# Binary cross-entropy on one core: a flat walk in 64 KiB runs over two SBUF rings, float32 results in place, every transfer on the GpSimd queue

## The chip, the cores and the metric

The kernel runs on one core of a Trainium2 chip. The metric is device time in microseconds (us), the median of several executions.

## The reference

```python
pred   = uniform(0.01, 0.99, (8192, 8192)).astype(float32)
target = randint(0, 2, (8192, 8192)).astype(float32)      # only 0.0 and 1.0

eps = 1e-7
pred = clip(pred, eps, 1 - eps)
out  = -(target * log(pred) + (1 - target) * log(1 - pred))
```

As the target is 0 or 1, the result is `-log|p - 1 + t|`: one logarithm is enough. Both kernels use that.

Two arrays of 268 MB are read and one of 268 MB is written: 805 MB in all, and very little arithmetic.

## The kernel before

It takes 64 blocks of 128 rows x 8192 columns. A row of a block is 32 KiB of contiguous float32. There are three buffers for pred, two for the target (cast to bf16 by the DMA) and two for the result (fp16, cast to float32 by the DMA).

```python
    def ops(bi, rows, r0, g0, t_p, t_t):
        t_o = pool_o.tile([P, F], fp16, name="t_o", tag="t_o")
        p_sl = t_p[:rows]
        nc.vector.scalar_tensor_tensor(               # p - 1 + t
            out=p_sl, in0=p_sl, scalar=1.0, in1=t_t[:rows], op0=sub, op1=add)
        nc.scalar.activation(out=p_sl, in_=p_sl, func=Square)
        nc.scalar.activation(out=p_sl, in_=p_sl, func=Ln)
        nc.vector.tensor_scalar(out=t_o[:rows], in0=p_sl, scalar1=-0.5, ...)
        # the store is put off: emit_store() issues it on gpsimd two blocks later

    def ops_tail(...):                                # the last two blocks, in 4 and 8 pieces
        ...                                           # same four ops, float32 in place
            nc.sync.dma_start(out=out_f[...], in_=p_sl)      # tail stores: SP queue

    for bi in range(n_blk):
        ...
        if big and bi == 0:
            nc.sync.dma_start(out=t_p[:rows], in_=pred_f[...])    # first pred load: SP queue
        else:
            nc.gpsimd.dma_start(out=t_p[:rows], in_=pred_f[...])
        nc.gpsimd.dma_start(out=t_t[:rows], in_=target_f[...])
        if bi - 2 in pending:
            emit_store(bi - 2)
        ...                                           # ops() or ops_tail()
```

Of the kernel before, what the change touches and what calls it, by code (L numbers as in the profile page):

```python
# [1 line left out]

# [4 lines left out]


@with_exitstack
def kernel(  # L10
    ctx: ExitStack,
    tc: tile.TileContext,
    pred: bass.AP,
    target: bass.AP,
    out: bass.AP,
):
    nc = tc.nc
    fp32 = mybir.dt.float32
    fp16 = mybir.dt.float16
    bf16 = mybir.dt.bfloat16  # L20

    P = nc.NUM_PARTITIONS

    pred_f = pred.flatten_outer_dims()
    target_f = target.flatten_outer_dims()
    out_f = out.flatten_outer_dims()

    R, C = pred_f.shape

    F = 8192 if C % 8192 == 0 else C  # L30
    n_col = C // F
    n_row = (R + P - 1) // P
    n_blk = n_row * n_col

    big = (R % P == 0) and n_blk >= 8 and F == 8192

    sub = mybir.AluOpType.subtract
    add = mybir.AluOpType.add
    mult = mybir.AluOpType.mult

    Square = mybir.ActivationFunctionType.Square
    Ln = mybir.ActivationFunctionType.Ln

    pool_p = ctx.enter_context(tc.tile_pool(name="bce_p", bufs=3 if big else 2))
    pool_t = ctx.enter_context(tc.tile_pool(name="bce_t", bufs=2))
    pool_o = ctx.enter_context(tc.tile_pool(name="bce_o", bufs=2))
    pool_w = ctx.enter_context(tc.tile_pool(name="bce_w", bufs=1))

    warm = pool_w.tile([1, 8], fp32, name="warm", tag="warm")
    nc.vector.memset(warm, 1.0)  # L50
    nc.scalar.activation(out=warm, in_=warm, func=Ln)  # L51

    lb = n_blk - 1
    slb = n_blk - 2

    pending: dict[int, list] = {}

    def emit_store(b: int, n: int | None = None):
        lst = pending[b]
        n = len(lst) if n is None else n  # L60
        for _ in range(n):
            dram, sl = lst.pop(0)
            nc.gpsimd.dma_start(out=dram, in_=sl)  # L63
        if not lst:
            del pending[b]

    def ops(bi, rows, r0, g0, t_p, t_t):
        t_o = pool_o.tile([P, F], fp16, name="t_o", tag="t_o")
        p_sl = t_p[:rows]
        nc.vector.scalar_tensor_tensor(  # L70
            out=p_sl, in0=p_sl, scalar=1.0, in1=t_t[:rows], op0=sub, op1=add
        )
        nc.scalar.activation(out=p_sl, in_=p_sl, func=Square)  # L73
        nc.scalar.activation(out=p_sl, in_=p_sl, func=Ln)  # L74
        nc.vector.tensor_scalar(  # L75
            out=t_o[:rows], in0=p_sl, scalar1=-0.5, scalar2=None, op0=mult
        )
        pending.setdefault(bi, []).append(
            (out_f[r0 : r0 + rows, g0 : g0 + F], t_o[:rows])
        )  # L80

    def ops_tail(rows, r0, g0, t_p, t_t, nchunk):
        W = F // nchunk
        for k in range(nchunk):
            c0 = k * W
            p_sl = t_p[:rows, c0 : c0 + W]
            nc.vector.scalar_tensor_tensor(  # L87
                out=p_sl,
                in0=p_sl,
                scalar=1.0,  # L90
                in1=t_t[:rows, c0 : c0 + W],
                op0=sub,
                op1=add,
            )
            nc.scalar.activation(out=p_sl, in_=p_sl, func=Square)  # L95
            nc.scalar.activation(out=p_sl, in_=p_sl, func=Ln)  # L96
            nc.vector.tensor_scalar(  # L97
                out=p_sl, in0=p_sl, scalar1=-0.5, scalar2=None, op0=mult
            )
            nc.sync.dma_start(  # L100
                out=out_f[r0 : r0 + rows, g0 + c0 : g0 + c0 + W], in_=p_sl
            )

    for bi in range(n_blk):
        i, j = divmod(bi, n_col)
        r0 = i * P
        rows = min(P, R - r0)
        g0 = j * F

        t_p = pool_p.tile([P, F], fp32, name="t_p", tag="t_p")  # L110
        t_t = pool_t.tile([P, F], bf16 if big else fp32, name="t_t", tag="t_t")

        if big and bi == 0:
            nc.sync.dma_start(out=t_p[:rows], in_=pred_f[r0 : r0 + rows, g0 : g0 + F])
        else:
            nc.gpsimd.dma_start(out=t_p[:rows], in_=pred_f[r0 : r0 + rows, g0 : g0 + F])  # L116
        nc.gpsimd.dma_start(out=t_t[:rows], in_=target_f[r0 : r0 + rows, g0 : g0 + F])  # L117

        s = bi - 2
        if s in pending:  # L120
            emit_store(s)

        if big and bi == slb:
            ops_tail(rows, r0, g0, t_p, t_t, 4)
        elif big and bi == lb:
            ops_tail(rows, r0, g0, t_p, t_t, 8)
        else:
            ops(bi, rows, r0, g0, t_p, t_t)

    for b in sorted(pending):  # L130
        emit_store(b)


# [1 line left out]
_INS = ['pred', 'target']  # L135
_OUTS = [((8192, 8192), 'float32')]


# [23 lines left out]
```

## Time and profile before

| | |
|---|---|
| time, median of 3 | 1867.4 us (1867.38 to 1867.72) |
| DMA, share of the 16 engines' span (GpSimd queue) | 99.9% |
| DVE / ACT busy | 45% / 48% |
| HBM traffic | 805 MB, 432 GB/s |

The first thing to read is the page's summary: busy time of the engines, the DMA row over 40 equal slices (each digit is tenths of busy time), and the queues (packets, MB, share of 16 engines).

```profile
DVE 841.3 (45%) x149; ACT 903.3 (48%) x150; POOL 100.9 (5%) x193
...
DMA  9999999999999999999999999999999999999999
...
q0 software_dynamic: 27216, 658.52, 99.9%
q1 hardware_dynamic: 1872, 12.58, 1.7%
...
HBM read 536.87 MB, written 268.44 MB: 432 GB/s over the span
```

DMA is full in every slice while the engines are idle half of the time. The queue `q0` is GpSimd's; `q1` is SP's. The MB of a queue are counted on the receiving side, so a cast target counts half (658.52 + 12.58 = 671.1 MB are 268.4 of pred, 134.2 of target in bf16 and 268.4 of result); the HBM line has the true bytes.

The packet records of the trace (start, duration and size of each DMA packet) show how full the engines are. I take the 16th packet after a given one for the next of the same engine: one packet takes 1226 ns (median), and the 16th starts 1209.5 ns later in a pred load, 1208 ns in a target load, 1207 ns in a store. All of these move 32 KiB on the float32 side, so the narrow side of these casts bought no DMA time. A transfer has 9 packets per engine: 8 rows and one 4-byte semaphore write (3024 packets of 4 bytes on this queue, 189 x 16). That is 27216 = 189 transfers x 16 x 9.

The end: these are busy times by window (us; busy us of DVE, ACT and POOL; clock; DMA share; GB/s).

```profile
1855.00:1860.00 5.00, 0.69 (x1) 1.24 (x2) 0.00 (x0) 1.00 1.02 419
1860.00:1865.00 5.00, 0.00 (x0) 0.00 (x0) 0.00 (x0) 1.00 0.57 231
1865.00:1865.70 0.70, 0.00 (x0) 0.00 (x0) 0.00 (x0) 1.00 0.00 0
```

DMA stays full until shortly before the end: the last data packet ends at 1863.95 us.

### The profile page before, as it was taken

The page shows a single profiled execution, that of the slowest core. Times are in us where ns is not written, and L with a number is a line of the kernel's source. Part 1 is how long each engine was busy: PE and PEld are TensorE (multiplying, and loading weights), DVE is VectorE, ACT ScalarE, POOL GpSimd, SP SyncE. Part 2 cuts the span into 40 slices and gives each one's busy share as a digit, 9 for nine tenths or more (in the row PEclk, how much of TensorE's full clock was granted, in tenths as well). Part 3 has the DMA queues.
Part 4 walks back from the last instruction along what each step waited for, and adds up shares of the span by engine and source line. Part 5 has one row for each costly group of instructions (what it writes and reads, how often), then busy time and mean ns, then how long its engine had stood idle before and what let it go on. Part 6 is the DMA issues. An engine that isn't in the chain of part 4 may idle for free.

```text
span 1865.7 us, 804 instructions
## 1 busy us (share of the span) xinstructions
DVE 841.3 (45%) x149; ACT 903.3 (48%) x150; POOL 100.9 (5%) x193
## 2 busy tenths in 40 slices
DVE  2645344453443534435344353453534535345353
ACT  3653644535445354453544635446354463553654
POOL 0000000000000000000000000000000000000000
DMA  9999999999999999999999999999999999999999
GB/s 325 338 377 353 351 379 344 375 356 347 384 341 376 356 346 387 344 368 363 343 388 345 364 369 341 390 344 360 371 343 386 344 359 372 347 379 352 352 378 351
DMA packets 29093, 671.14 MB, mean 360 GB/s; under 512 B 3232, under 2 KB 3232, under 8 KB 4256
## 3 DMA queue, kind: packets, MB, share of 16 engines
q0 software_dynamic: 27216, 658.52, 99.9%
q1 hardware_dynamic: 1872, 12.58, 1.7%
q14 instruction: 5, 0.04, 0.0%
HBM read 536.87 MB, written 268.44 MB: 432 GB/s over the span
## 4 chain that ended last, share of the span: by engine, by line
DMA 80%; issue 14%; ACT 2%; DVE 2%; another core or an unknown queue 1%; POOL 0%; POOLq 0%; DVEq 0%; PEldq 0%
DMA t_t<-in_target_dram 80%; DVE t_p L70 1%; ACT t_p L96 1%; ACT t_p L95 1%; DVE t_o L75 0%; ACT t_p L73 0%; ACT t_p L74 0%; DVE t_p L87 0%; DVE t_p L97 0%; POOL t_p L116 0%; POOL out_dram L63 0%; POOLq L117 0%; POOL t_t L117 0%; POOLq L63 0%
## 5 line engine op out<-in xcount | busy, mean ns | idle before, releaser
L73 ACT ACTIVATE t_p<-t_p 128x8192 f32<-128x8192 f32 x62 | 435.8, 7029 | 923.6 <-DVE t_p L70 923.6
L75 DVE TENSOR_SCALAR t_o<-t_p 128x8192 f16<-128x8192 f32 x62 | 274.4, 4427 | 845.0 <-ACT t_p L74 845.0
L70 DVE SCALAR_TENSOR_TENSOR t_p<-t_p,t_t 128x8192 f32<-128x8192 f32 x62 | 538.9, 8693 | 144.8 <-DMA t_t<-in_target_dram 144.8
L74 ACT ACTIVATE t_p<-t_p 128x8192 f32<-128x8192 f32 x62 | 435.8, 7029 | 2.0
L63 POOL DMA_DIRECT2D out_dram<-t_o x62 | 33.4, 538 | 1121.9 <-DVE t_o L75 1101.2
L117 POOL DMA_DIRECT2D t_t<-in_target_dram x64 | 34.1, 533 | 581.5 <-DVE t_p L70 580.7
L116 POOL DMA_DIRECT2D t_p<-in_pred_dram x63 | 33.9, 537 | 0.3 <-issue 0.3
L95 ACT ACTIVATE t_p<-t_p 128x1024 f32<-128x1024 f32 (+1 forms) x12 | 15.6, 1327 | 26.5 <-DVE t_p L87 26.5
L87 DVE SCALAR_TENSOR_TENSOR t_p<-t_p,t_t 128x1024 f32<-128x1024 f32 (+1 forms) x12 | 18.4, 1575 | 17.2 <-DMA t_t<-in_target_dram 17.2
L96 ACT ACTIVATE t_p<-t_p 128x1024 f32<-128x1024 f32 (+1 forms) x12 | 15.6, 1330 | 0.1
L97 DVE TENSOR_SCALAR t_p<-t_p 128x1024 f32<-128x1024 f32 (+1 forms) x12 | 10.3, 868 | 7.9 <-ACT t_p L96 7.9
L51 ACT ACT_TABLE_LOAD x1 | 1.3, 1283 | 0.7 <-PEq L146 0.7
L50 DVE MEMSET warm<- 1x8 f32 x1 | 0.1, 65 | 0.8 <-PEq L146 0.8
L51 ACT ACTIVATE warm<-warm 1x8 f32<-1x8 f32 x1 | 0.2, 208 | 0.0
L146 POOL MEMSET const-float32-0.0<- 128x1 f32 x1 | 0.1, 100 | 0.2 <-issue 0.2
L146 POOL MEMSET const-bfloat16-1.0<- 128x1 bf16 x1 | 0.1, 102 | 0.0
L146 POOL MEMSET const-float32-1.0<- 128x1 f32 x1 | 0.1, 100 | 0.0
L146 POOL MEMSET const-uint8-127<- 128x1 uint8 x1 | 0.1, 100 | 0.0
## 6 DMA issues: line engine op xcount, KB each, us to landing
t_p<-in_pred_dram POOLq DMA_DIRECT2D x63, 4096.0 KB, 49.3
out_dram<-t_o POOLq DMA_DIRECT2D x62, 4096.0 KB, 40.1
t_t<-in_target_dram POOLq DMA_DIRECT2D x64, 2048.0 KB, 49.0
t_p<-in_pred_dram SPq DMA_DIRECT2D x1, 4096.0 KB, 19.6
out_dram<-t_p SPq DMA_DIRECT2D x4, 1024.0 KB, 27.3
out_dram<-t_p SPq DMA_DIRECT2D x8, 512.0 KB, 8.5
```

The costliest lines, as they stand in the source:

```text
L51: nc.scalar.activation(out=warm, in_=warm, func=Ln)
L63: nc.gpsimd.dma_start(out=dram, in_=sl)
L70: nc.vector.scalar_tensor_tensor(out=p_sl, in0=p_sl, scalar=1.0, in1=t_t[:rows], op0=sub, op1=add)
L73: nc.scalar.activation(out=p_sl, in_=p_sl, func=Square)
L74: nc.scalar.activation(out=p_sl, in_=p_sl, func=Ln)
L75: nc.vector.tensor_scalar(out=t_o[:rows], in0=p_sl, scalar1=-0.5, scalar2=None, op0=mult)
L87: nc.vector.scalar_tensor_tensor(out=p_sl, in0=p_sl, scalar=1.0, in1=t_t[:rows, c0 : c0 + W], op0=sub, op1=add,)
L95: nc.scalar.activation(out=p_sl, in_=p_sl, func=Square)
L96: nc.scalar.activation(out=p_sl, in_=p_sl, func=Ln)
L97: nc.vector.tensor_scalar(out=p_sl, in0=p_sl, scalar1=-0.5, scalar2=None, op0=mult)
L116: nc.gpsimd.dma_start(out=t_p[:rows], in_=pred_f[r0 : r0 + rows, g0 : g0 + F])
L117: nc.gpsimd.dma_start(out=t_t[:rows], in_=target_f[r0 : r0 + rows, g0 : g0 + F])
```

## The change

The intent: fewer and longer transfers (64 KiB runs where there were 32 KiB rows), no separate result buffer (float32 results in place, which also drops the fp16 rounding), the clip that the reference asks for, and one queue that holds all transfers in an order written by hand. The arrays are walked as flat memory. A chunk of width w is 128 runs of w elements, one per partition; widths go 4096, 4096, 8192, then 30 x 16384, then 8192, 4096, 2048, 1024, 1024. The ring for pred has 32768 columns, so it holds two large chunks.

```diff
+RING = 32768
+SUB = 2048
+    head = [4096, 4096, 8192]
+    tail = [8192, 4096, 2048, 1024, 1024]
+    big = 16384
 ...
+    ring_p = pool.tile([P, RING], fp32, name="ring_p", tag="ring_p")
+    ring_t = pool.tile([P, RING], bf16, name="ring_t", tag="ring_t")
 ...
+    def load(k):
+        c, w = at(k), widths[k]
+        nc.gpsimd.dma_start(out=ring_t[:, c : c + w], in_=dram(target_f, cols[k], w))
+        nc.gpsimd.dma_start(out=ring_p[:, c : c + w], in_=dram(pred_f, cols[k], w))
+    def store(k):
+        c, w = at(k), widths[k]
+        nc.gpsimd.dma_start(out=dram(out_f, cols[k], w), in_=ring_p[:, c : c + w])
+    def front(c, w):
+        p, t = ring_p[:, c : c + w], ring_t[:, c : c + w]
+        nc.vector.tensor_scalar(out=p, in0=p, scalar1=EPS, scalar2=1 - EPS, op0=Alu.max, op1=Alu.min)
+        nc.vector.scalar_tensor_tensor(out=p, in0=t, scalar=1.0, in1=p, op0=Alu.subtract, op1=Alu.add)
+        nc.scalar.activation(out=p, in_=p, func=Act.Abs)
+        nc.scalar.activation(out=p, in_=p, func=Act.Ln)
+    def back(c, w):
+        p = ring_p[:, c : c + w]
+        nc.vector.tensor_scalar(out=p, in0=p, scalar1=-1.0, scalar2=None, op0=Alu.mult)
+    def compute(k):                 # sub-chunks of SUB columns: front(i), then back(i - 1)
 ...
+    with tc.manual_schedule():
+        for k in range(len(widths)):
+            while loaded < len(widths):          # load while the ring has room; store first to make room
 ...
+            compute(k)
-    (all of ops, ops_tail, emit_store, the pools, and the first load and the tail stores on nc.sync)
```

In steady state GpSimd issues store k-1 (after the last DVE op of chunk k-1), then target load k+1 (no wait that matters), then pred load k+1, which has to wait until store k-1 has **landed**, because it overwrites that place in the ring.

More of the change, by code (lines that the diff above doesn't have):

```diff
@@ L4, with chunk_widths @@
 import concourse.tile as tile
-from concourse import bass_utils, mybir
+from concourse import mybir
 from concourse._compat import with_exitstack
+EPS = 1e-7
+RING = 32768
+SUB = 2048
+def chunk_widths(total):
+    head = [4096, 4096, 8192]
+    tail = [8192, 4096, 2048, 1024, 1024]
+    big = 16384
+    n = (total - sum(head) - sum(tail)) // big
+    widths = head + [big] * n + tail
+    assert sum(widths) == total
+    return widths
 @with_exitstack
@@ L18 @@
     fp32 = mybir.dt.float32
-    fp16 = mybir.dt.float16
     bf16 = mybir.dt.bfloat16
+    Alu = mybir.AluOpType
+    Act = mybir.ActivationFunctionType
     P = nc.NUM_PARTITIONS
-    pred_f = pred.flatten_outer_dims()
-    target_f = target.flatten_outer_dims()
-    out_f = out.flatten_outer_dims()
-    R, C = pred_f.shape
-    F = 8192 if C % 8192 == 0 else C
-    n_col = C // F
-    n_row = (R + P - 1) // P
-    n_blk = n_row * n_col
-    big = (R % P == 0) and n_blk >= 8 and F == 8192
-    sub = mybir.AluOpType.subtract
@@ L38 @@
-    add = mybir.AluOpType.add
-    mult = mybir.AluOpType.mult
-    Square = mybir.ActivationFunctionType.Square
-    Ln = mybir.ActivationFunctionType.Ln
-    pool_p = ctx.enter_context(tc.tile_pool(name="bce_p", bufs=3 if big else 2))
-    pool_t = ctx.enter_context(tc.tile_pool(name="bce_t", bufs=2))
-    pool_o = ctx.enter_context(tc.tile_pool(name="bce_o", bufs=2))
-    pool_w = ctx.enter_context(tc.tile_pool(name="bce_w", bufs=1))
-    warm = pool_w.tile([1, 8], fp32, name="warm", tag="warm")
@@ L50 @@
-    nc.vector.memset(warm, 1.0)
-    nc.scalar.activation(out=warm, in_=warm, func=Ln)
-    lb = n_blk - 1
-    slb = n_blk - 2
-    pending: dict[int, list] = {}
-    def emit_store(b: int, n: int | None = None):
-        lst = pending[b]
-        n = len(lst) if n is None else n
-        for _ in range(n):
-            dram, sl = lst.pop(0)
-            nc.gpsimd.dma_start(out=dram, in_=sl)
-        if not lst:
-            del pending[b]
-    def ops(bi, rows, r0, g0, t_p, t_t):
-        t_o = pool_o.tile([P, F], fp16, name="t_o", tag="t_o")
-        p_sl = t_p[:rows]
+    R, C = pred.shape
@@ new lines, with dram @@
+    pred_f = pred.rearrange("r c -> (r c)")
+    target_f = target.rearrange("r c -> (r c)")
+    out_f = out.rearrange("r c -> (r c)")
+    total = R * C // P
+    def dram(flat, col, w):
+        return flat[col * P : (col + w) * P].rearrange("(p w) -> p w", p=P)
+    pool = ctx.enter_context(tc.tile_pool(name="rings", bufs=1))
+    ring_p = pool.tile([P, RING], fp32, name="ring_p", tag="ring_p")
+    ring_t = pool.tile([P, RING], bf16, name="ring_t", tag="ring_t")
+    warm = pool.tile([1, 8], fp32, name="warm", tag="warm")
@@ new lines, with at @@
+    nc.vector.memset(warm, 1.0)
+    nc.scalar.activation(out=warm, in_=warm, func=Act.Ln)
+    widths = chunk_widths(total)
+    cols = [sum(widths[:k]) for k in range(len(widths))]
+    def at(k):
+        c = cols[k] % RING
+        assert c + widths[k] <= RING
+        return c
+    def load(k):
+        c, w = at(k), widths[k]
+        nc.gpsimd.dma_start(out=ring_t[:, c : c + w], in_=dram(target_f, cols[k], w))
+        nc.gpsimd.dma_start(out=ring_p[:, c : c + w], in_=dram(pred_f, cols[k], w))
@@ L70, in ops @@
+    def store(k):
[3 more added lines that the diff above has]
+        p, t = ring_p[:, c : c + w], ring_t[:, c : c + w]
+        nc.vector.tensor_scalar(
+            out=p, in0=p, scalar1=EPS, scalar2=1 - EPS, op0=Alu.max, op1=Alu.min
+        )
         nc.vector.scalar_tensor_tensor(
-            out=p_sl, in0=p_sl, scalar=1.0, in1=t_t[:rows], op0=sub, op1=add
+            out=p, in0=t, scalar=1.0, in1=p, op0=Alu.subtract, op1=Alu.add
@@ L72, in ops @@
         )
-        nc.scalar.activation(out=p_sl, in_=p_sl, func=Square)
-        nc.scalar.activation(out=p_sl, in_=p_sl, func=Ln)
+        nc.scalar.activation(out=p, in_=p, func=Act.Abs)
+        nc.scalar.activation(out=p, in_=p, func=Act.Ln)
+    def back(c, w):
+        p = ring_p[:, c : c + w]
         nc.vector.tensor_scalar(
-            out=t_o[:rows], in0=p_sl, scalar1=-0.5, scalar2=None, op0=mult
+            out=p, in0=p, scalar1=-1.0, scalar2=None, op0=Alu.mult
         )
-        pending.setdefault(bi, []).append(
-            (out_f[r0 : r0 + rows, g0 : g0 + F], t_o[:rows])
-        )
@@ L82, in ops_tail @@
-    def ops_tail(rows, r0, g0, t_p, t_t, nchunk):
-        W = F // nchunk
-        for k in range(nchunk):
-            c0 = k * W
-            p_sl = t_p[:rows, c0 : c0 + W]
-            nc.vector.scalar_tensor_tensor(
-                out=p_sl,
-                in0=p_sl,
-                scalar=1.0,
-                in1=t_t[:rows, c0 : c0 + W],
-                op0=sub,
-                op1=add,
-            )
-            nc.scalar.activation(out=p_sl, in_=p_sl, func=Square)
-            nc.scalar.activation(out=p_sl, in_=p_sl, func=Ln)
-            nc.vector.tensor_scalar(
-                out=p_sl, in0=p_sl, scalar1=-0.5, scalar2=None, op0=mult
-            )
-            nc.sync.dma_start(
-                out=out_f[r0 : r0 + rows, g0 + c0 : g0 + c0 + W], in_=p_sl
-            )
@@ L104 @@
-    for bi in range(n_blk):
-        i, j = divmod(bi, n_col)
-        r0 = i * P
-        rows = min(P, R - r0)
-        g0 = j * F
-        t_p = pool_p.tile([P, F], fp32, name="t_p", tag="t_p")
-        t_t = pool_t.tile([P, F], bf16 if big else fp32, name="t_t", tag="t_t")
-        if big and bi == 0:
-            nc.sync.dma_start(out=t_p[:rows], in_=pred_f[r0 : r0 + rows, g0 : g0 + F])
-        else:
-            nc.gpsimd.dma_start(out=t_p[:rows], in_=pred_f[r0 : r0 + rows, g0 : g0 + F])
-        nc.gpsimd.dma_start(out=t_t[:rows], in_=target_f[r0 : r0 + rows, g0 : g0 + F])
-        s = bi - 2
-        if s in pending:
-            emit_store(s)
-        if big and bi == slb:
-            ops_tail(rows, r0, g0, t_p, t_t, 4)
-        elif big and bi == lb:
-            ops_tail(rows, r0, g0, t_p, t_t, 8)
-        else:
-            ops(bi, rows, r0, g0, t_p, t_t)
@@ L130 @@
-    for b in sorted(pending):
-        emit_store(b)
+    def compute(k):
+        c, w = at(k), widths[k]
+        n = max(1, w // SUB)
+        s = w // n
+        for i in range(n):
+            front(c + i * s, s)
+            if i:
+                back(c + (i - 1) * s, s)
+        back(c + (n - 1) * s, s)
+    with tc.manual_schedule():
+        stored = loaded = 0
+        for k in range(len(widths)):
+            while loaded < len(widths):
+                end = cols[loaded] + widths[loaded]
+                while stored < k and end > cols[stored] + RING:
+                    store(stored)
+                    stored += 1
+                if end > cols[stored] + RING:
+                    break
+                load(loaded)
+                loaded += 1
+            compute(k)
+        while stored < len(widths):
+            store(stored)
+            stored += 1
```

## The prediction

> **What bounds the kernel now.** The DMA engines. The page's queue section gives the GpSimd queue 99.9% of the 16 engines' span; the 40-slice row of DMA shows 9 in every slice. DVE is 45% busy and ACT 48%. HBM moves 805 MB (537 read, 268 written), 432 GB/s over the span. In the timeline, a 128x8192 block repeats every 29.04 us: 12.58 MB, 433 GB/s. The packet records show why nothing is left inside: each engine starts a 32 KiB packet every 1209.5 ns (pred load, plain), 1208 ns (target load, cast to bf16) and 1207 ns (store, fp16 cast to f32), without gaps, and a whole load-load-store round costs only about 40 ns beyond its 24 packets per engine. That is 27.1 GB/s per engine, 434 GB/s in all. [...] All three directions pay for the wider (float32, HBM) side, so the casts to two bytes save no DMA time.
>
> **What the change does.** HBM bytes stay the same: pred and target read, out written in float32. The store reads float32 instead of fp16 in SBUF; by the pitches above (plain 1209.5, cast 1207) this neither helps nor hurts.
> - Descriptors double to 64 KiB and DMAs halve (192 to about 114). [...]
> - DVE gains a clip. A 128x2048 float32 tensor_scalar took 1.23 us, the two-input op 2.29: 256 x (1.23 + 2.29 + 1.23) = 1.21 ms, 65% of the span. ACT stays near 0.96 ms (Abs in place of Square, 1.9 us each). Both stay off the path.
> - In place with a ring of two big chunks: pred load k+2 waits until store k has landed. In queue order, target load k+2 (19 us of transfer) stands between them and covers that. A 16384-wide chunk needs about 42 us of compute after its load; the DMA queue then holds store, target load and pred load of neighbours, 58 us. So about 15 us slack: no starvation expected.
> - Head: before, the first data packet (SP queue) ran at 1.7 us, the first of the GpSimd queue only at 6.1 us. After, everything goes through GpSimd: up to 4 us lost.
> - Tail: before, DMA was full until 1862.2 us, packets of 4 KiB slightly slower. After, I work out from the durations that stores are ready just in time; the last 1024-wide chunks run serially (about 5 us each), costing 0 to 3 us of DMA idleness.
>
> **Sum.** 32 rounds of 58.0 us = 1855 to 1859, plus 3 to 6 us before the first data, 1 to 3 us in the tail, 2 us to the end: span about 1864, time about 1866 us (time was 1.7 above span). Predicted 1866, range 1858 to 1876; faster by over 2% 0.02, within 2% 0.95, slower 0.03.
>
> **What would show it.** DMA still 9 in all slices, 99%; chunks every 58.0 us; DVE waits for pred loads rather than the reverse; GpSimd's pred loads wait for stores but the packet records show no gap; DVE near 65%; first data packet at 3 to 6 us.
>
> **What would make it wrong.** 64 KiB descriptors running at a different rate[...]; chunk compute longer than 58 us; a gap in the queue at each store-to-load wait.

The sum came to a span of about 1864 us and a time of about 1866 us. Twice the measured 29.04 us is a round of 58.08 us, 32 of these are 1859 us, the upper end of "1855 to 1859". "Slightly slower", of the 4 KiB packets in the tail before, is in numbers one start every 156 ns (26.3 GB/s an engine) and 420 GB/s in all between 1858 and 1860 us.

## More of the kernel before

A timeline has start, duration, what, and in brackets the idle time before and who ended it.

```profile
1058.90 0.53 POOL L117 DMA_DIRECT2D t_t<-in_target_dram  x1 [9.38 <-DVE t_p L70]
1080.06 0.55 POOL L63 DMA_DIRECT2D out_dram<-t_o  x1 [20.63 <-issue]
1080.60 0.54 POOL L116 DMA_DIRECT2D t_p<-in_pred_dram  x1
...
1106.53 0.54 POOL L63 DMA_DIRECT2D out_dram<-t_o  x1 [18.05 <-DVE t_o L75]
```

The other stores in mid-run come 18.05 us after the issue before them and 0.30 us after their DVE op. One single store comes 20.63 us after, released by nothing that the profile shows. I passed over it when I predicted. It is the 114th transfer on the GpSimd queue, and it comes back below.

## The result, and the profile after

| | before | after |
|---|---|---|
| time, median of 4 | 1867.51 us | 1870.43 us (1870.25 to 1870.78) |
| ratio | | 1.0016, 95% interval 1.0002 to 1.003 |
| span of the profile | 1865.7 us | 1868.8 us |
| first data packet / last data packet ends | 1.74 / 1863.95 us | 2.64 / 1867.30 us |

A ratio is the mean time of one kernel's fast runs over that of the other's from the same measuring rounds, so it is not quite the ratio of the medians. By the 2% limit the two kernels are the same. The 3 us that were lost are clear of noise, and so the question is where a change with which the fastest DMA engine needs 0.20% less time (58.085 to 57.967 us a round, below) lost its gain, and 3 us more.

The summary lines of the page after:

```profile
DVE 1178.6 (63%) x772; ACT 976.3 (52%) x516; POOL 65.4 (3%) x118
...
DMA  9999999999999999999999999999999999999998
...
q0 software_dynamic: 16416, 671.10, 99.9%
...
HBM read 536.87 MB, written 268.44 MB: 431 GB/s over the span
```

DVE rose from 45 to 63% (the clip) and nothing came of it: DMA is still full, except in the last slice. The waits (engine, line, what it waited for: us in total, times, longest us):

```profile
POOL ring_p L75 <- DMA out_dram<-ring_p: 1084.9, 30, 37.1
...
POOL out_dram L79 <- DVE ring_p L94: 689.9, 36, 25.7
DVE ring_p L83 <- DMA ring_p<-in_pred_dram: 552.9, 32, 18.8
```

GpSimd waits 30 times for a store to land before it issues a pred load (36 us each), and yet the DMA engines do not fall idle: by the packet records the 16 engines are idle 6.8 us on average over the whole run, of which 6.2 us lie after 1840 us. DVE waits for loads, not the reverse. So the loss is not in the middle. The windows at the end, which answer to those of before:

```profile
1855.00:1860.00 5.00, 2.52 (x3) 2.35 (x3) 0.53 (x1) 1.00 0.79 331
1860.00:1865.00 5.00, 0.69 (x1) 1.12 (x2) 0.25 (x1) 1.00 0.12 51
1865.00:1868.80 3.80, 0.00 (x0) 0.00 (x0) 0.29 (x1) 1.00 0.34 138
```

For about 7 us DMA is nearly empty. And the timeline of the tail's GpSimd issues and last DVE ops:

```profile
1843.65 1.22 DVE L83 TENSOR_SCALAR ring_p<-ring_p 128x2048 f32<-128x2048 f32 x1
...
1844.03 0.96 POOL L79 DMA_DIRECT2D out_dram<-ring_p  x1 [11.39 <-DVE ring_p L94]
...
1857.40 0.53 POOL L79 DMA_DIRECT2D out_dram<-ring_p  x1 [4.23 <-DVE ring_p L94]
...
1861.18 0.69 DVE L94 TENSOR_SCALAR ring_p<-ring_p 128x1024 f32<-128x1024 f32 x1 [2.21 <-ACT ring_p L90]
...
1864.75 0.54 POOL L79 DMA_DIRECT2D out_dram<-ring_p  x1 [6.82 <-issue]
```

The last store is issued 2.88 us after its DVE op ended at 1861.87, where the one before it took 0.30 us; again "issue" is named, that is, nothing that the profile shows. It is again the 114th transfer on the queue.

The packet records hold one more thing. Every transfer ends with one semaphore write per engine. The time from the first to the last of these 16 writes is how far apart the 16 engines are; I call it the *spread*. From 200 to 1700 us it never fell by more than 0.001 us from one transfer to a later one, before or after: the lag of the last engine behind the first stayed.

| spread of the 16 DMA engines, us, at | 100 | 300 | 700 | 1100 | 1700 us |
|---|---|---|---|---|---|
| before | 0.62 | 0.62 | 0.95 | 1.14 | 1.63 |
| after | 0.92 | 3.10 | 4.07 | 5.02 | 6.38 |

Counted over 26 or 27 rounds of 25.2 MB from 200 us on (a round is two blocks before, one chunk after), the fastest engine needs 58.085 us a round before and 57.967 after: this is the gain of long runs, 0.118 us, 3.8 us over 32 rounds (in the control below the fastest needs 57.996, which would be 2.8 us). The slowest engine needs 58.123 before and 58.126 after: it gains nothing. The kernel ends with the slowest.

The spread does not grow evenly. Of the 85 packets of 64 KiB in the kernel after that took over 2480 ns (2418 is usual), 76 start before 870 us. From there to 1700 us the spread grows from 4.4 to 6.4 us, nearly all of it in three steps of 0.49, 0.68 and 0.68 us, at 1028, 1318 and 1608 us. Each step comes at most 10 us after a fetch of instructions, an 8 KiB transfer of about 0.3 us on a queue of its own (1018, 1311 and 1606 us). So the spread grew here along with two things, slow packets early and fetches later. The kernel after has 11 such fetches in its run, the kernel before 5.

So the spans differ by +3.1 us: +0.90 first data, +2.45 from first to last data packet, -0.28 from there to the end. The middle term is no gain on the slowest engine, plus the late last store: the slowest engine was done with all else at 1864.76 us and needed 1.24 us more, so 1.3 us of the 1867.30 are lateness of the store; the rest, 1.15 us, is left over. The engines were 1.45 us further apart already at 200 us (2.07 against 0.62); that this is the rest was not tested.

### The profile page after: what moved, and what is told of

Its sections match the earlier page's. It is cut to its first block, busy times and chain, and to the rows that moved or that the text cites. A ratio compares the mean times of both kernels' runs of the same rounds, so it can differ in the third digit from the quotient of the medians.

```text
span 1868.8 us, 1563 instructions
## 1 busy us (share of the span) xinstructions
DVE 1178.6 (63%) x772; ACT 976.3 (52%) x516; POOL 65.4 (3%) x118
## 3 DMA queue, kind: packets, MB, share of 16 engines
q0 software_dynamic: 16416, 671.10, 99.9%
## 4 chain that ended last, share of the span: by engine, by line
DMA 34%; issue 30%; DVE 27%; ACT 7%; POOL 1%; another core or an unknown queue 1%; POOLq 0%; PEldq 0%
DMA ring_p<-in_pred_dram 32%; DVE ring_p L86 13%; DVE ring_p L94 7%; DVE ring_p L83 7%; ACT ring_p L89 3%; ACT ring_p L90 3%; DMA out_dram<-ring_p 2%; POOL out_dram L79 1%; POOL ring_t L74 1%; POOL ring_p L75 0%; POOLq L151 0%; POOLq L79 0%; PEldq L151 0%
## 5 line engine op out<-in xcount | busy, mean ns | idle before, releaser
L89 ACT ACTIVATE ring_p<-ring_p 128x2048 f32<-128x2048 f32 (+1 forms) x257 | 488.9, 1902 | 876.0 <-DVE ring_p L86 876.0
L83 DVE TENSOR_SCALAR ring_p<-ring_p 128x2048 f32<-128x2048 f32 (+1 forms) x257 | 312.9, 1218 | 552.9 <-DMA ring_p<-in_pred_dram 552.9
L86 DVE SCALAR_TENSOR_TENSOR ring_p<-ring_t,ring_p 128x2048 f32<-128x2048 bf16 (+1 forms) x257 | 586.9, 2284 | 8.8
L90 ACT ACTIVATE ring_p<-ring_p 128x2048 f32<-128x2048 f32 (+1 forms) x257 | 489.2, 1903 | 8.1
L94 DVE TENSOR_SCALAR ring_p<-ring_p 128x2048 f32<-128x2048 f32 (+1 forms) x257 | 313.1, 1218 | 120.8 <-ACT ring_p L90 120.8
L75 POOL DMA_DIRECT2D ring_p<-in_pred_dram x38 | 21.9, 576 | 1094.1 <-DMA out_dram<-ring_p 1084.9
L79 POOL DMA_DIRECT2D out_dram<-ring_p x38 | 22.1, 581 | 700.3 <-DVE ring_p L94 689.9
L74 POOL DMA_DIRECT2D ring_t<-in_target_dram x38 | 21.8, 574 | 5.3 <-DMA ring_t<-in_target_dram 4.4
```

The source lines that it names most:

```text
L74: nc.gpsimd.dma_start(out=ring_t[:, c : c + w], in_=dram(target_f, cols[k], w))
L75: nc.gpsimd.dma_start(out=ring_p[:, c : c + w], in_=dram(pred_f, cols[k], w))
L79: nc.gpsimd.dma_start(out=dram(out_f, cols[k], w), in_=ring_p[:, c : c + w])
L83: nc.vector.tensor_scalar(out=p, in0=p, scalar1=EPS, scalar2=1 - EPS, op0=Alu.max, op1=Alu.min)
L86: nc.vector.scalar_tensor_tensor(out=p, in0=t, scalar=1.0, in1=p, op0=Alu.subtract, op1=Alu.add)
L89: nc.scalar.activation(out=p, in_=p, func=Act.Abs)
```

## The experiments

The twelve runs ask four things. Is the ring's wait really hidden, and how much slack has DVE? What is the late 114th transfer? What does it cost to end on the GpSimd queue? Why do the engines drift apart?

### Control

> The changed kernel once more, as a control beside the others on one chip. Every theory: 1870.4 us, 2.5 to 3.2 us over the kernel before; first GpSimd data packet at 2.6 us; the 114th and last GpSimd transfer issued about 2.9 us after the DVE op it waits for.

Measured: 1870.79 us (1869.12 to 1871.82, 5 runs), ratio 1.0017. First data at 2.65 us; the last store 2.88 us after its DVE op; spread at 1700 us 5.53.

### Does the target load hide the store-to-load wait?

```diff
     def load(k):
-        nc.gpsimd.dma_start(out=ring_t[...], in_=dram(target_f, cols[k], w))
         nc.gpsimd.dma_start(out=ring_p[...], in_=dram(pred_f, cols[k], w))
+        nc.gpsimd.dma_start(out=ring_t[...], in_=dram(target_f, cols[k], w))
```

> The changed kernel with the pred load issued before the target load of the same chunk. The pred load waits until the store of the chunk before last has landed, and now nothing stands between that store and it in the queue. Theory (the target load is what hides the ring's store-to-load wait): all 16 DMA engines fall idle about 3.1 us once in each of some 30 rounds [...]: 1955 to 1975 us; and because the engines meet again at each such gap, they no longer drift apart (spread under 1.5 us). Rival (the wait was never a risk, the queue holds enough): within 5 us of 1870.

Measured: 2000.4 us (one run, its state is unknown, but the effect is 30 times the difference studied). A round takes 62.49 us, 4.5 us more; all 16 engines stand idle together 30 times, 2.1 us on average and 3.1 at most. That is 61 us of the 130; idleness of single engines adds about 13. The rest is packets that took longer: they fill 96.2% of 1998.6 us, 1923 us an engine, where the changed kernel's fill 99.9% of 1868.8, 1867 us. Why they took longer is not shown. The spread at 1700 us is 0.7 us. The line of the queue on its page, and the line of the wait:

```profile
q0 software_dynamic: 16416, 671.10, 96.2%
```

```profile
POOL ring_p L74 <- DMA out_dram<-ring_p: 1263.3, 30, 43.6
```

The theory holds in kind and is wrong in size. I expected gaps of 3.1 us and so 95 us more. Most gaps are 1.86 us (0.63 from the last byte to the issue, 0.53 for the issue, 0.70 to the first packet), and the longer packets, which I had not foreseen, made it 130 us. The order "target, then pred" in the changed kernel is worth 130 us. The wait of 36 us per chunk cost nothing there because 19 us of another transfer (8 packets of 2418 ns an engine) stood in the queue behind the store. With 30 idle moments the engines were also 0.7 us apart at 1700 us, where the changed kernel's were 6.38, as expected.

### How much slack has a chunk's compute?

```diff
+        nc.vector.tensor_scalar(... same clip ...)
+        nc.vector.tensor_scalar(... same clip ...)
         nc.vector.tensor_scalar(
             out=p, in0=p, scalar1=EPS, scalar2=1 - EPS, op0=Alu.max, op1=Alu.min)
```

> The clip done three times in place of once: 513 more DVE ops of 1.22 us, 626 us more DVE work. The result is the same. Theory (a chunk's compute of 41 us has 15 to 17 us of slack within a round of 58 us): the compute of a chunk grows by 19.5 us to 60 us, just past the round, so the kernel becomes DVE-bound and takes 1915 to 1950 us, not 1870 + 626. Rival (DVE [...] is already on the path): 2200 us or more.

Measured: 1984.5 us (one run), 114 us for 624 us of added DVE work. A round takes 60.8 us, as expected (a chunk's compute of 60 us is the new limit). The total is 35 us above my range: I had forgotten that a DVE-bound kernel still has the tail's compute to do when its loads are in; the DMA engines are idle 36 us after 1920 us.

```profile
DVE 1802.6 (91%) x1286; ACT 980.3 (49%) x516; POOL 91.1 (5%) x118
...
q0 software_dynamic: 16416, 671.10, 95.5%
```

So the one clip of the change (40.3 us of compute in a round of 58) lies in the slack. So do the GpSimd issues that grow longer beside DVE's work. In the tail timeline above, the store issue at 1844.03 takes 0.96 us, not 0.53, and ends at 1844.99, 0.12 us after the DVE op that it overlapped. All seven lengthened issues of the changed kernel (0.96 to 1.48 us) end 0.12 us after a one-input DVE op (`tensor_scalar`), while the 35 issues that lie wholly under the two-input op took the usual 0.53 us. By what one holds up the other is not shown, and words of mine about that are cut from the expectation above. Where the ops are twice as long, in the last experiment below (c3, after c2), the store issues are longer too. The lines give minimum/median/maximum in ns, first for c2 and then for c3:

```profile
L82 POOL DMA_DIRECT2D out_dram<-ring_t x33: 536/958/1413, 25.0 to 1809.9; - x33
```

```profile
L82 POOL DMA_DIRECT2D out_dram<-ring_t x33: 538/2026/2496, 25.0 to 1808.9; - x33
```

In these kernels the queue held other work, and c3 is the fastest of all. In e4, where it held none, five of the 30 gaps were 2.9 to 3.1 us instead of 1.9, because the issue took 1.4 us or more.

### What is the late last store?

```diff
-    head = [4096, 4096, 8192]
+    head = [8192, 8192]
```

> Head of two chunks of 8192 in place of three; the tail is untouched, but the GpSimd queue carries 111 transfers, not 114. Theory: the late last store is a stall that comes with the 114th transfer on the GpSimd queue (in the kernel before it is also the 114th that is 2.6 us late, in mid-run, where the queue hides it). Then no issue here is late: the last store is issued 0.2 to 0.4 us after its DVE op, and the span is 1 to 2.6 us shorter, 1866.2 to 1867.8. Rival: the last store waited for the slowest DMA engine to finish the store before it, which ended at that very moment. Then it is again issued 2 us or more late and the span stays within 0.5 us of 1868.8.

Measured: 1874.62 us (1874.03 to 1875.24), ratio 1.0038. Half of the theory held: the last store is issued 0.30 us after its DVE op, and the last data packet ends at 1865.87, 1.4 us sooner. The rival is out. But the kernel became 4 us slower than the control. The instruction records of the end say why. These are the counts and durations (minimum/median/maximum, ns) of GpSimd's drain instructions, first for the changed kernel and then for this one:

```profile
L151 POOLq DRAIN  x3: 51/89/3299, 1864.7 to 1868.5; - x3
```

```profile
L151 POOLq DRAIN  x3: 51/81/9684, 1862.0 to 1872.1; - x3
```

The drain that closes GpSimd's program takes 9.68 us here and ends 5.8 us after the last data packet, where the changed kernel's ends 0.7 us after. Neither theory had foreseen that.

Over all profiles, the lateness is exact. Nine of them have at least 114 transfers on the GpSimd queue. In eight (the kernel before, the changed kernel and its control, and five experiments) the 114th comes 2.87 to 2.88 us after its DVE op, other stores come after 0.3. In the ninth (the 32 KiB runs below) the store had no DVE op to wait for any more; it begins 2.58 us after the issue before it, where its neighbours begin at once. So the delay is the same 2.6 us in all nine. Why it is the 114th is not shown, nor what the drain waits for. What the runs show: kernels whose last GpSimd transfer was the 114th drain 0.7 us after the last byte, those with other counts 4.4 to 5.8 us after.

### The tail stores on the SP queue

```diff
-        nc.gpsimd.dma_start(out=dram(out_f, cols[k], w), in_=ring_p[:, c : c + w])
+        q = nc.sync if w < 8192 and k > 8 else nc.gpsimd
+        q.dma_start(out=dram(out_f, cols[k], w), in_=ring_p[:, c : c + w])
```

> The four tail stores narrower than 8192 go through the SP queue (they need no cast); 110 transfers on GpSimd. Theory (tail: late issue plus GpSimd start-up plus serial compute): the last data packet ends at 1863 to 1865 in place of 1867.3, span 1864.5 to 1866.5, so 2.5 to 4 us less than the changed kernel. Rival (the end is set by the DMA engine that drifted furthest, 5 to 6 us behind): at most 1.3 us less.

Measured: 1869.68 us (1868.93 to 1869.86), 1.1 us under the control. The rival is right: the semaphores of the last three stores arrive at intervals of 1.25 us, the time that one engine needs for its 8 packets of one such store (in the tail before, 4 KiB packets of an engine started every 156 ns). A single engine, over 6 us behind, works them off alone.

### The kernel before, with its tail on the GpSimd queue

```diff
-            nc.sync.dma_start(
+            nc.gpsimd.dma_start(
                 out=out_f[r0 : r0 + rows, g0 + c0 : g0 + c0 + W], in_=p_sl
```

> The kernel before with its 12 tail stores on the GpSimd queue, not on SP. Theory (when the last transfer is on the GpSimd queue, GpSimd's closing drain ends 4 to 6 us after the last byte, where the SP route needs 1.7 us): span +3 to +6 us, the drain the last to end. Rival (the long drain belonged to the in-place ring): within 1.5 us of the kernel before.

Measured: 1879.25 us (1879.14 to 1879.59), ratio 1.0063, 11.7 us slower, twice what was expected. 4.6 us of it are the wind-down that was in question: from the last data packet to the end it takes 6.3 us, not 1.7. This kernel has no ring: the longer wind-down came with the queue. The other 7.2 us are another cost of one queue: the last pred load now stands behind four tail stores that wait for DVE, and is issued 49 us later than in the kernel before. First the kernel before, then this one:

```profile
1775.72 0.54 POOL L116 DMA_DIRECT2D t_p<-in_pred_dram  x1
```

```profile
1824.88 0.54 POOL L116 DMA_DIRECT2D t_p<-in_pred_dram  x1
```

The DMA engines are idle 3.9 us between 1800 and 1830 us, where those of the kernel before are never idle, and all that follows is later.

### Is it the 64 KiB runs that make the engines drift?

```diff
-    big = 16384
+    big = 8192
```

> Chunks of 8192 in the middle: 32 KiB runs, four chunks in the ring, twice the transfers; the 114th transfer falls in mid-run. Theory (a fixed cost per packet and per transfer, so long runs gain 0.2%): the fastest DMA engine needs 58.08 us per 25.2 MB in place of 57.96, over the run +3 to +4 us; the end stall goes, -1.3 us: 1871 to 1873 us in all. Rival (64 KiB packets are what lets the 16 engines drift apart and so cost the tail): drift at most 2 us and time at or below that of the changed kernel, 1867 to 1870.

Measured: 1879.85 us (1877.65 to 1880.72), ratio 1.0063. Neither expectation was met. The fastest engine needs 58.163 us a round, more than in the kernel before, and the spread at 1700 us is 6.3 us. So 64 KiB runs are not needed for the drift, and with short runs this schedule is even slower; why its fastest engine too is slower than that of the kernel before is not shown. The drain ends 4.4 us after the last byte.

### Is it the order of the transfers?

In the packet records of the changed kernel, the delays cluster at one place in the round: at the last packets of a pred load, before a store begins. At 253 us all 16 of these last packets took 2487 to 3659 ns, where 2418 is usual. In the kernel before, a store follows a target load. So I gave the kernel before the same neighbours:

```diff
+        nc.gpsimd.dma_start(out=t_t[:rows], in_=target_f[...])
         ...                                           # pred load
-        nc.gpsimd.dma_start(out=t_t[:rows], in_=target_f[...])
```

> The kernel before with the target load issued before the pred load, so that a store follows a pred load in the queue, as in the changed kernel. Theory of the drift (the last pred packets are slowed when the first store packets of other engines start, which only this order has): the 16 engines end 4 us or more apart, in place of 1.9, and the time rises by 1 to 4 us. Rival (the drift comes from 64 KiB packets or from instruction fetches): spread under 2.5 us and the time within 1 us of the kernel before.

Measured: 1867.61 us, ratio 1.0000; spread at 1700 us 1.53. My theory is wrong: the order alone does nothing.

### Is it the plain float32 store?

The same kernel, with one more line changed:

```diff
-        t_o = pool_o.tile([P, F], fp16, name="t_o", tag="t_o")
+        t_o = pool_o.tile([P, F], fp32, name="t_o", tag="t_o")
```

> The kernel before with the target load first (b1) and a float32 result tile, so that the store no longer casts: the float32 half of the change alone, with 32 KiB rows. Theory of the drift (the plain float32 store, behind a pred load, disturbs the last pred packets): the 16 engines end 4 us or more apart and the fastest engine still needs 58.08 us per 25.2 MB; time +1 to +5 us. Rival (the drift comes from the ring, its distances in memory or its many instructions): spread under 2.5 us, time within 1 us of the kernel before.

Measured: 1873.06 us (1872.75 to 1873.35), ratio 1.0029, interval 1.0016 to 1.0043. The spread at 1700 us is 7.18 us. The slowest engine needs 58.264 us a round, the fastest 58.092. Against b1 nothing differs but the element type of the result in SBUF: no ring, no clip, no 64 KiB runs, the same transfers in the same order. The instruction fetches (5 in the run) and the time of the DVE op that writes the result (4.43 us) are the same too; the result's tile takes twice the room in SBUF. The float32 result alone makes the engines drift, and costs this kernel 5.5 us. The HBM bytes are the same; only the cast is gone. The drift is not a steady rate: the spread reaches 7.08 us at 642 us and is still 7.18 at 1700, so the 58.264 us is a mean of a slow start and an undisturbed rest. Why it stops is open. Whether it does so too where a store follows a target load was not tried, and by which mechanism the packets are held up stays open.

### Other ends for the changed kernel

```diff
     def load(k):                        # first pred load on SP
+        q = nc.sync if k == 0 else nc.gpsimd
     def store(k):                       # five tail stores on SP
+        q = nc.sync if k >= TAIL else nc.gpsimd
+    def compute_tail():                 # one pipeline over the tail's sub-chunks:
+        ...                             # front(next), then back(previous), across chunks
```

> The changed kernel with other ends: the first pred load and the five tail stores on SP, and the tail's sub-chunks in one DVE pipeline. Theory (start-up, GpSimd's wind-down and the serial tail cost the changed kernel its gain; the drift stays): first data at 1.7 us, DVE done by 1857 us, span 1865 to 1867.5, the last bytes those of one or two DMA engines 5 to 6 us behind the rest. If the ends were of no account: 1868 to 1869.5 as before.

Measured: 1868.51 us (1867.65 to 1868.69), ratio to the kernel before 1.0003 (0.999 to 1.0017), span 1866.8, first data at 1.75 us, last DVE op over at 1849.5. As expected: about 2.6 us come from the ends (ratio 1.0017 for the control; the three changes of this run were not tried apart), and the drift stays (spread 6.39 at 1700 us).

### Casting stores in the ring

c1, with the results of all but the tail written as fp16 into the target's place in its ring. Now it is the target load that waits for the store to land, so pred is loaded first.

```diff
-    ring_t = pool.tile([P, RING], bf16, name="ring_t", tag="ring_t")
+    ring_t = pool.tile([P, RING], fp16, name="ring_t", tag="ring_t")
 ...  # load(): pred, then target; store(): from ring_t, in the tail from ring_p
     def back(c, w, ring=ring_p):
-        nc.vector.tensor_scalar(out=p, in0=p, scalar1=-1.0, ...)
+        nc.vector.tensor_scalar(out=ring[:, c : c + w], in0=p, scalar1=-1.0, ...)
```

> c1 with the results of all but the tail written as fp16 into the target's place in its ring (so stores cast again, as in the kernel before, and the target load, not the pred load, waits for the store). Theory (the plain float32 store is what makes the engines drift; 64 KiB runs alone gain 0.2%): spread under 2.5 us, 57.97 us per 25.2 MB, span 1860 to 1863, so 0.15 to 0.3% faster than the kernel before. Rival (drift from the ring or the instructions): spread 4 us or more and the time of c1.

Measured: 1866.47 us (1866.38 to 1866.7), ratio 0.9994 (0.9982 to 1.0007), span 1864.5. The fastest engine needs 57.955 us a round, as expected. The spread at 1700 us is 4.10, not under 2.5; but the mean of the engines is only 0.59 us behind the fastest, where c1 has 1.74. So most engines keep together now and few are far behind. The 2 us against c1 on the same chip are the effect; as the load order changed with it, they are not the cast's alone for certain. Four of the spread's steps are of 0.7 us, and these lie at the times of instruction fetches: the DMA records hold 12 fetches of 8 KiB during the run, about 0.3 us each.

### Fewer instructions

```diff
-        n = max(1, w // SUB)
+        n = max(1, w // (2 * SUB if w == 16384 else SUB))
```

> c2 with sub-chunks of 4096 in the 30 large chunks: 120 sub-chunks there in place of 240, so about half the DVE and ACT instructions; the DMAs are the same. Theory (what is left of the drift in c2 comes from instruction fetches, which take some 0.3 us each from one DMA engine): the fetches during the run fall from 12 to 6 or 7, the spread of the engines from 4.1 to 2 to 2.8 us, span 1862.5 to 1864.0. Rival (the rest of the drift belongs to the ring): spread 3.5 us or more, span as c2, 1864.5.

Measured: 1865.08 us (1865.01 to 1865.5), ratio 0.9987 (0.9973 to 1.0001), span 1862.9. The fetches during the run fall to 7. The spread is 2.58 us at 1700 us and 3.25 after one more fetch at 1771 us: a little above the expected range, below the rival's. The slowest engine now needs 58.015 us a round. Its last windows, in the columns of those shown above:

```profile
1855.00:1858.00 3.00, 0.00 (x0) 0.00 (x0) 0.00 (x0) 1.00 1.00 414
1858.00:1860.00 2.00, 0.00 (x0) 0.00 (x0) 0.00 (x0) 1.00 0.37 150
1860.00:1862.00 2.00, 0.00 (x0) 0.00 (x0) 0.00 (x0) 1.00 0.05 20
```

DMA is full to 1858 us and one engine trails. This version beats both kernels by their medians, by 2.6 us and 5 us. Against the kernel before that is 0.14%, and the interval just includes 1; the 5 us are across chips.

The runs side by side (spread at 1700 us; fastest and slowest engine per 25.2 MB):

| kernel | store | runs | spread, us | fastest / slowest, us | time, us |
|---|---|---|---|---|---|
| before | cast | 32 KiB | 1.63 | 58.085 / 58.123 | 1867.5 |
| b1: store after pred load | cast | 32 KiB | 1.53 | 58.085 / 58.126 | 1867.6 |
| b3: b1 with float32 result | plain | 32 KiB | 7.18 | 58.092 / 58.264 | 1873.1 |
| e3: changed kernel, short runs | plain | 32 KiB | 6.33 | 58.163 / 58.301 | 1879.9 |
| after | plain | 64 KiB | 6.38 | 57.967 / 58.126 | 1870.4 |
| c1: other ends | plain | 64 KiB | 6.39 | 57.962 / 58.116 | 1868.5 |
| c2: c1 with fp16 result | cast | 64 KiB | 4.10 | 57.955 / 58.083 | 1866.5 |
| c3: c2 with half the instructions | cast | 64 KiB | 2.58 | 57.955 / 58.015 | 1865.1 |

## Why the prediction was right or wrong

The verdict (within 2%) and the range (1858 to 1876) hold; the central value, 1866, is 4.4 us too low. Point by point:

- **The bound.** Right. DMA is full before and after, and triple clip shows that DVE had the slack claimed for it ("about 42 us of compute", "about 15 us slack": measured 40.3 of 58 us).
- **The hidden wait.** Right. "Target load k+2 stands between them and covers that": without it, +130 us.
- **The gain of long runs.** In the sum it is what takes 32 rounds from 1859 us down to 1855. Measured, the fastest engine gained 0.20%, 3.8 us. But the step "the store reads float32 instead of fp16 in SBUF; this neither helps nor hurts" failed. The pitch of one packet is indeed the same (the fastest engine needs 58.092 us a round in b3, 58.085 in b1); I took from it that the transfer as a whole is the same. b3 shows +5.5 us for just that step, by engines that drift apart, and in the changed kernel the drift used up the whole gain: 58.126 us a round on the slowest engine, 58.123 before. There the store is not the only source: bringing the cast back (c2) saved 2 us, larger ops with fewer instruction fetches (c3, on another chip) 1.4 us more, and the prediction had no term for the fetches of its many small ops. The term that was mis-sized is "32 rounds of 58.0 us = 1855 to 1859": 32 rounds of the slowest engine's 58.126 are 1860, and from first to last data it took 1864.7 us, the tail included.
- **The head.** "3 to 6 us before the first data" was too much: 2.64 us, 0.9 later than before. I had read the 6.1 us of GpSimd's first packet in the kernel before as its start-up. It stood behind SP's packets on the same engines: in the changed kernel, with no load on SP, the first packet comes 1.37 us after the start of the first issue. From 6.1 us on the packets of the two queues alternate (of SP at 4.9, of GpSimd at 6.1, of SP at 7.3, of GpSimd at 8.5 us); why three of SP ran on each engine before GpSimd's first is not shown. This error was luck for the total: with the measured head the sum would have come to about 1864 us, 6 us too low.
- **The tail.** "0 to 3 us of DMA idleness" missed two costs that the kernel before had hidden or avoided: the 114th transfer comes 2.6 us late and is now the very last one, and a kernel that ends on the GpSimd queue may end with that queue's wind-down (e1: 5.8 us after the last byte; b2: 4.6 us lost). The kernel before ended on SP.
- **What I named as risks.** 64 KiB runs at another rate: only 0.2% faster on the fastest engine. A risk about DVE and GpSimd is cut from the text; measured, seven GpSimd issues took 0.96 to 1.48 us, not 0.53, beside DVE ops, harmless here. The drift was not among the risks.

## What to carry to other kernels

When all DMA engines are full, look at the slowest of them and not at the mean: from b1 to b3 the fastest engine's time per round stayed the same (58.085 and 58.092 us) while the engines came to stand 7.18 us apart, not 1.53, and the kernel ended 5.5 us later, with the last. Try the first load and the last stores off the GpSimd queue: in c1 this, with the tail in one pipeline, was worth about 2.6 us, and in b2 tail stores on GpSimd cost 11.7 us. Give every load that waits for a store another transfer to hide behind (e4: without it, +130 us). A profile's single unexplained wait in mid-run is worth a look before one reorders the queue, since the reordering can move it to the end (the 114th transfer, 2.6 us).
